# Seven products instead of eight in the down projection of both MLPs of a two-layer trunk, with new rooms for its operands and groups of 4, 4, 3 and 3 pairs

## The chip, the cores and the metric

The kernel runs on one core of one Trainium2 chip. The metric is the device time of one execution in microseconds; lower is better. The median of three runs before the change is 2502.86 us (2498.45 to 2505.21).

## The reference

The model is one step of a two-layer encoder over 1024 prompt rows and 32 sample rows (T = 1056 rows of D = 1024 columns). Layer 0 has an mLSTM mixer, layer 1 band attention over shared keys and values, and each layer has an MLP with a squared ReLU. All of it is in float32. Cut to what matters here:

```python
for l in range(DEPTH):                       # DEPTH = 2
    sh1, sc1, g1, sh2, sc2, g2 = jnp.split(ada_mod(c, p['w_ada'][l], p['b_ada'][l])[:, None, :], 6, axis=-1)
    u = x * (1 + sc1) + sh1
    ...
    x = layer_norm(ALPHA * x + (1 + g1) * y, p['ln_g'][l, 0], p['ln_b'][l, 0])
    u = x * (1 + sc2) + sh2
    f = jnp.square(jax.nn.relu(u @ p['w_up'][l])) @ p['w_down'][l]
    x = layer_norm(ALPHA * x + (1 + g2) * f, p['ln_g'][l, 1], p['ln_b'][l, 1])
```

`w_up[l]` is 1024 by 4096 and `w_down[l]` 4096 by 1024. `ada_mod` is the conditioning: silu(c) times a weight of 1024 by 6144 for each layer, for the prompt's and the sample's condition.

## The kernel before, in words

Data lie transposed: 128 features on the partitions, the 1056 rows along the free axis. A float32 product is made of three matmuls on values split into a high and a low part (`proj`, L118 high by high, L119 high by low, L120 low by high). `split` makes the two parts: ScalarE copies the high part (L89), VectorE subtracts for the low one (L90). Weights come from DRAM through three "raw" buffers and become split weights in six "wc" buffers of the pool `ring`; VectorE and ScalarE make them.

An accumulator holds the residual stream. In layer 0 it is three tiles of 384, 384 and 288 rows (`acc`, the blocks `TBS`); in layer 1 it is one tile (`ACC`). `add_gated_at` (L963) takes a finished PSUM bank, multiplies it by the gate and adds it to the accumulator, on VectorE. It makes one instruction for each piece of the accumulator and for each side of the border between prompt and sample, which lies at row 1024.

`Flow` runs side work in small steps: generators such as `norm` (a layer norm with its modulation) and `ada_rest` yield the number of ticks until their next step, and the main work calls `flow.tick` after each tile. `ada_rest` computes layer 1's conditioning while layer 0's MLP runs, in 32 pairs of 128 columns: for each pair two loads of 512 KB into raw buffers, 16 operations on VectorE (L238, L241), a transposition (L245) and a reduction (L246). The delays between its steps are `ADA_B`.

Layer 0's MLP (`mlp`) goes by 8 groups of 512 hidden features. In turn it makes `up` for a group (L1000 to L1003: ReLU and square, then the split into `h`) and `down` (four k blocks of the group, then `add_gated_at` into `acc`). It takes the rows in the three blocks of `TBS`, and the last group ends block by block, so that the next norm can begin.

Layer 1's MLP is written out by itself and takes down in another way. The rows are four quarters of 264 (`QN`), in two pairs `tp`; the hidden features are 16 pairs of 128-wide blocks. For 14 of them (`NW`) a two-by-two product of blocks (two quarters of rows, two blocks of hidden features, two blocks of outputs) is made with seven block products instead of eight (`PRODS`), from sums and differences of the blocks:

- `up_tile` puts ReLU and square of four tiles into `H` and makes the seven forms of the moving operand, split, in `HL`, of which there is one buffer. Two DMAs write HL to DRAM (`hd`).
- `forms` loads a block of `w_down` and makes the seven forms of the weights.
- `unit` is one group of pairs and one pair of outputs `m`: for each product 3 x kg matmuls of 264 columns (L1568) into one of three PSUM banks for a pair of quarters, and after each product an addition into the accumulator. The bank goes on collecting after that addition. Where `m` is 0 or 3 the two pairs of quarters follow each other, else they take turns.
- `load_f` (L1551) loads a form of the moving operand from `hd` into its room, 14 rooms in all; at `m == 3` it loads the next group's form after each product.

Groups have 3, 4, 4 and 3 pairs. The first group begins with extra units, because nine of its fourteen rooms come only after `HL`'s pool is closed. The last two pairs of hidden features are taken in the plain way at the end, block by block, with the final norm behind each block.

The order of TensorE's instructions in the attention and in layer 1's units is as written (`manual_schedule`); elsewhere, and on the other engines everywhere, a scheduler orders the instructions when the program is built. All loads and stores are issued by SyncE, in one queue.

Of the kernel before, what the change touches and what calls it, by code (L numbers as in the profile page):

```python
# [15 lines left out]
P = 128  # L16
# [59 lines left out]
def trunk_kernel(ctx: ExitStack, tc: tile.TileContext, a, o):  # L76
# [736 lines left out]
    ADA_B = (4.0, 2.0, 1.0)  # L813
# [7 lines left out]
    def make_layer(acc, pp, uo, usegs=segs):  # L821
# [4 lines left out]
        def norm(ti, ni, nm, w, affine=True, after=None):  # L826
# [48 lines left out]
            for i in range(0, KC, 2):  # L875
                nc.vector.tensor_mul(x[:, i:i + 2], x[:, i:i + 2], w2[:, 0:1].broadcast_to([P, 2, n]))
                for k in (i, i + 1):
                    for off, m, cnd in usegs(t0, n):
# [3 lines left out]
                                 tmp[:, :m], nc.scalar)  # L882
# [98 lines left out]
        def mlp(hp, l, gate, order, before_tb, after_tb, last):  # L981
            w_up, w_dn = a["w_up"][l], a["w_down"][l]
            NG = 8
            hs = {}
            wups = {}

            def up_w(g, pr):
                if (g, pr) not in wups:
                    wups[g, pr] = [wblock(f"up{l}_{g}_{pr}_{i}", w_up, 512 * i, g * 512 + pr * 256) for i in range(2)]
                return wups[g, pr]  # L990

            def up(g, c, ti):
                t0, n = TBS[ti]
                ps = mm(f"up_{l}_{g}_{c}_{t0}")
                proj(ps[:, :n], n, up_w(g, c // 2), c % 2, lambda hl, k: uo(hl, k, t0, n))
                if (g, c) not in hs:
                    hs[g, c] = hp.tile([P, 2, T], F32R, tag="h", name=f"h_{l}_{g}_{c}", bufs=5)
                ht = hs[g, c]
                r = tmp_t([P, 384], f"r_{l}_{g}_{c}_{t0}")[:, :n]
                nc.scalar.activation(r, ps[:, :n], AF.Relu)  # L1000
                nc.scalar.activation(ht[:, 0, t0:t0 + n], r, AF.Square)
                nc.vector.tensor_mul(r, r, r)
                nc.vector.tensor_sub(ht[:, 1, t0:t0 + n], r, ht[:, 0, t0:t0 + n].bitcast(F32))  # L1003
                flow.tick(n / 96)

            def down(g, w, fc, t0, n):
                ps = mm(f"dn_{l}_{g}_{fc}_{t0}")
                proj(ps[:, :n], n, [w], fc % 2, lambda hl, k: hs[g, k][:, hl, t0:t0 + n])
                add_gated_at(t0, n, ps, gate, fc)
                flow.tick(n / 192)  # L1010

            for pr in range(2):
                up_w(0, pr)
            early = set()
            for i, ti in enumerate(order):
                if i == 2:
                    for t in order[:EARLY]:
                        up(1, 0, t)
                        early.add(t)
                before_tb(ti)  # L1020
                for c in range(4):
                    up(0, c, ti)
            for g in range(NG):
                if g + 1 < NG:
                    for ti in order:
                        if g or ti not in early:
                            up(g + 1, 0, ti)
                if g < NG - 1:
                    for pr in range(4):
                        w = wblock(f"dn{l}_{g}_{pr}", w_dn, g * 512, pr * 256)  # L1030
                        for fc in (2 * pr, 2 * pr + 1):
                            for ti in order:
                                down(g, w, fc, *TBS[ti])
                    if g < NG - 2 or last is not TBS:
                        for c in range(1, 4):
                            for ti in order:
                                up(g + 1, c, ti)
                else:
                    ws = []

                    def finish(blk):
                        for fc in range(KC):
# [4 lines left out]
                    if last is TBS:  # L1047
# [4 lines left out]
                        for c, ti in ((3, 1), (2, 2), (3, 2)):  # L1052
                            up(g, c, ti)
# [632 lines left out]
```

## Time and profile before

| | |
|---|---|
| median of three runs | 2502.86 us |
| the profiled execution, its own time | 2503.12 us |
| its span, first to last instruction | 2501.3 us |
| granted TensorE clock, mean | 0.991 |
| layer 0's MLP, on TensorE | 516.0 to 1264.6 us |
| layer 1's up | 1732.2 to 2113.9 us |
| layer 1's units of seven products | 2113.7 to 2432.8 us |
| layer 1's plain rest of down and the last norm | to the end |

The profile is that of one execution. Busy time of an engine says how much of a stretch it worked; whether it sets the end is read from what the other engines wait for there. A matmul's own duration is longer than the distance between two of them, because they are pipelined; so TensorE's pace is read from how many matmuls a stretch without idle time holds.

### The profile page before, as it was taken

To read this page: it belongs to the slowest core of one execution; us is meant where nothing else is said; L and a number is where in the kernel's file an instruction comes from. 1 tells how busy PE (TensorE), PEld (TensorE's weight loads), DVE (VectorE), ACT (ScalarE), POOL (GpSimd) and SP (SyncE) were. 2 spreads that over 40 slices of the span, in tenths; PEclk is the share of its full clock that TensorE was granted. 3 is DMA by queue.
4 is the path that set the end of the run, shared out by engine and by line. 5 is a ranking of instruction groups with operands and counts; after the bars stand their busy time and mean duration, and the time that the engine had idled before them with its cause. 6 is when DMAs were issued, how large, how long until landed. Compare 5 with 4: busy or idle time off the path is not lost.

```text
span 2501.3 us, 42666 instructions
## 1 busy us (share of the span) xinstructions
PE 2418.5 (97%) x16844; PEld 2315.5 (93%) x16844; DVE 1755.0 (70%) x4033; ACT 1040.4 (42%) x2185; POOL 167.4 (7%) x315
## 2 busy tenths in 40 slices
PE   7999999999999999999999899998999999989997
PEld 4999999999999999999999877798999999889997
DVE  4899998778778768766696667737644442766678
ACT  4644455481221221221375566737944443211122
POOL 0211100000000000000001144400000000000003
PEclk9999999999999999999999999999999999999999
DMA  8433234313324323333123400051486667567552
GB/s 295 120 109 100 84 90 132 98 35 118 92 87 126 93 90 121 93 93 115 59 89 94 107 1 2 18 146 43 149 261 209 213 200 247 179 239 285 185 177 70
DMA packets 256108, 316.78 MB, mean 127 GB/s; under 512 B 11160, under 2 KB 233516, under 8 KB 251812
## 3 DMA queue, kind: packets, MB, share of 16 engines
q1 hardware_dynamic: 255908, 314.07, 38.7%
q8 instruction: 132, 2.16, 0.4%
q14 instruction: 68, 0.56, 0.1%
HBM read 241.48 MB, written 74.91 MB: 126 GB/s over the span
## 4 chain that ended last, share of the span: by engine, by line
PE 78%; DVE 7%; DMA 6%; ACT 3%; issue 1%; POOL 0%; SPq 0%; DVEq 0%; ACTq 0%; POOLq 0%
PE up L118 10%; PE up L119 10%; PE up L120 10%; PE dn L1568 8%; PE dn L119 5%; PE dn L118 5%; PE dn L120 5%; PE pv L1308 2%; PE pt L1288 2%; PE s L1258 2%; DMA fx_w<-hd 2%; DMA fx<-hd 1%; PE o L118 1%; PE o L119 1%; PE o L120 1%
## 5 line engine op out<-in xcount | busy, mean ns | idle before, releaser
L1568 PE MATMUL dn<-fx,wf 128*128 128x264 f32 x2184 | 276.7, 286 | 21.0 <-DMA fx<-hd 12.7
L1568 PEld LDWEIGHTS dn<-fx,wf 128*128 128x128 f32 x2184 | 270.4, 190 | 25.8 <-issue 10.9
L119 PE MATMUL up<-u,w_up 128*128 128x264 f32 x1024 | 290.8, 285 | 0.6 <-DVE u L331 0.6
L120 PE MATMUL up<-u,w_up 128*128 128x264 f32 x1024 | 290.0, 285 | 0.0
L118 PE MATMUL up<-u,w_up 128*128 128x264 f32 x1024 | 289.1, 286 | 0.2 <-ACT w_up L89 0.2
L119 PE MATMUL dn<-h,w_dn 128*128 128x384 f32 (+1 forms) x768 | 249.5, 325 | 0.0
L118 PE MATMUL up<-U,w_up 128*128 128x384 f32 (+1 forms) x768 | 249.2, 324 | 0.0
L119 PE MATMUL up<-U,w_up 128*128 128x384 f32 (+1 forms) x768 | 247.9, 323 | 0.0
L118 PE MATMUL dn<-h,w_dn 128*128 128x384 f32 (+1 forms) x768 | 247.8, 323 | 0.0
L120 PE MATMUL up<-U,w_up 128*128 128x384 f32 (+1 forms) x768 | 247.6, 322 | 0.0
L120 PE MATMUL dn<-h,w_dn 128*128 128x384 f32 (+1 forms) x768 | 247.3, 322 | 0.0
L963 DVE SCALAR_TENSOR_TENSOR ACC<-dn,ada,ACC 128x264 f32<-128x264 f32 (+5 forms) x328 | 133.1, 427 | 105.5 <-PE dn L1568 96.6
L119 PEld LDWEIGHTS up<-u,w_up 128*128 128x128 f32 x1024 | 194.5, 190 | 1.1 <-DVE u L331 1.1
L118 PEld LDWEIGHTS up<-u,w_up 128*128 128x128 f32 x1024 | 193.4, 190 | 0.6 <-ACT w_up L89 0.6
L120 PEld LDWEIGHTS up<-u,w_up 128*128 128x128 f32 x1024 | 193.3, 189 | 0.3 <-DVE w_up L90 0.3
L238 DVE SCALAR_TENSOR_TENSOR aacc<-rada,cs,aacc 128x256 f32<-128x256 f32 x448 | 190.3, 477 | 0.0
L963 DVE SCALAR_TENSOR_TENSOR acc<-dn,ada,acc 128x384 f32<-128x384 f32 (+2 forms) x256 | 119.3, 486 | 47.0 <-PE dn L120 45.9
L1000 ACT ACTIVATE r<-up 128x384 f32<-128x384 f32 (+1 forms) x96 | 44.2, 462 | 244.5 <-PE up L120 236.7
L119 PEld LDWEIGHTS dn<-h,w_dn 128*128 128x128 f32 x768 | 144.5, 188 | 0.2 <-DVE h L1003 0.2
L120 PEld LDWEIGHTS dn<-h,w_dn 128*128 128x128 f32 x768 | 144.5, 188 | 0.0
L120 PEld LDWEIGHTS up<-U,w_up 128*128 128x128 f32 x768 | 144.3, 188 | 0.0
L118 PEld LDWEIGHTS up<-U,w_up 128*128 128x128 f32 x768 | 144.2, 188 | 0.1
(350 smaller groups left out, 5986.6 us busy)
## 6 DMA issues: line engine op xcount, KB each, us to landing
hd<-HL SPq DMA_DIRECT2D x56, 924.0 KB
rada<-in_w_ada_dram SPq DMA_DIRECT2D x64, 512.0 KB
raw_up<-in_w_up_dram SPq DMA_DIRECT2D x64, 512.0 KB
fx<-hd SPq DMA_DIRECT2D x26, 1056.0 KB
fx<-hd SPq DMA_DIRECT2D x26, 792.0 KB
raw_dn<-in_w_down_dram SPq DMA_DIRECT2D x36, 512.0 KB
ada_room<-in_w_ada_dram SPq DMA_DIRECT2D x32, 512.0 KB
rada<-in_w_ada_kv_dram SPq DMA_DIRECT2D x16, 512.0 KB
```

The costliest lines, as they stand in the source:

```text
L118: nc.tensor.matmul(ps, wh, mov(0, k), start=(k == 0), stop=False)
L119: nc.tensor.matmul(ps, wh, mov(1, k), start=False, stop=False)
L120: nc.tensor.matmul(ps, wl, mov(0, k), start=False, stop=(k == nk - 1))
L238: nc.vector.scalar_tensor_tensor(acc[:, cnd], raw[:, k], sc, acc[:, cnd], op0=ALU.mult, op1=ALU.add)
L963: nc.vector.scalar_tensor_tensor(xs, ps[:, off + o:off + o + mm_], gate[:, fc, cnd:cnd + 1], xs, op0=ALU.mult, op1=ALU.add)
L1000: nc.scalar.activation(r, ps[:, :n], AF.Relu)
L1258: nc.tensor.matmul(s[:, b, :w], qst, kk[i][:, g, k0 + j0:k0 + j0 + w], start=(i == 0), stop=(i == 1))
L1288: nc.tensor.transpose(pt[:kp, j - j0, pr * P:(pr + 1) * P], ps_[pr][:, j * P:j * P + kp], ident)
L1308: nc.tensor.matmul(pv[64 * e:64 * e + 64, :nq], V[:kp, vt0 + j, g * 64:(g + 1) * 64], pts[e][:kp, j, :nq], start=(j == 0), stop=(j == nt - 1))
L1568: nc.tensor.matmul(p, ws[w][:, wl, k], x[:, xl, k], start=first and k + n_ == 0, stop=k == kg - 1 and n_ == 2, skip_group_check=not first)
```

## The change

A function `mlp7` takes the place of `mlp` and of layer 1's written-out MLP, and both layers use it, through classes `L0` and `L1` that tell it their operands and accumulators. `ADA_B` grows, and the low part of a modulation is made from a VectorE product in layer 1. `PRODS`, `forms` and `up_tile` are as before, apart from names; `up_plain` makes the last two pairs without `H` and `HL`. Cut to its core:

```diff
-    ADA_B = (4.0, 2.0, 1.0)
+    ADA_B = (5.0, 2.5, 1.0)
...
-                                 tmp[:, :m], nc.scalar)
+                                 tmp[:, :m], nc.scalar if usegs is segs else None)
...
-        def mlp(hp, l, gate, order, before_tb, after_tb, last):
...
+    GRP = [(0, 4), (4, 4), (8, 3), (11, 3)]
...
+    class Room:
+        def mov(self, hl, k):
+            return self.t[:, hl, k] if self.pieces is None else self.pieces(hl, k // 2)[:, k % 2 * QN:(k % 2 + 1) * QN]
+        def load(self, src, kg):
+            if self.pieces is None:
+                nc.sync.dma_start(self.t[:, :, :kg].bitcast(F32), src)
+                return
+            for hl in range(2):
+                for k in range(0, kg, 2):
+                    n = min(2, kg - k)
+                    nc.sync.dma_start(self.pieces(hl, k // 2)[:, :n * QN].bitcast(F32),
+                                      src[:, hl, k:k + n].rearrange("p k t -> p (k t)"))
+
+    def mlp7(L):
...
+        def up_plain(pb, tp):
+            for f in range(2):
+                r = tmp_t([P, 2, QN], f"hr{l}_{pb}_{f}_{tp}")
+                for i in range(2):
+                    nc.scalar.activation(r[:, i], up_mm(pb, f, 2 * tp + i), AF.Relu)
+                    flow.tick(QN / 96)
+                nc.vector.tensor_mul(r, r, r)
+                hl = ring.tile([P, 2, 2, QN], F32R, tag="raw", name=f"hl{l}_{pb}_{f}_{tp}", bufs=3)
+                split(hl[:, 0], hl[:, 1], r)
+                nc.sync.dma_start(hpl[2 * (pb - NW) + f, :, :, 2 * tp * QN:2 * (tp + 1) * QN],
+                                  hl.bitcast(F32).rearrange("p l q t -> p l (q t)"))
+        tp0, tp1 = L.pairs
+        for pb in range(2):
+            up_w(pb)
+        for i in range(2):
+            L.ready(i)
+            for pb in range(2):
+                for f in range(2):
+                    up_tile(pb, f, L.quarters[i])
+        up_unit(2, tp0)
+        L.ready(2)
+        for pb in range(3):
+            up_unit(pb, tp1)
+        for pb in range(3, NW):
+            for tp in L.pairs:
+                up_unit(pb, tp)
+        hh_cm.__exit__(None, None, None)
+        f4_cm = tc.tile_pool(name=f"f4{l}", bufs=1, reuse_waits="tile")
+        f4p = f4_cm.__enter__()
...
+        def unit(g, m, phases, ws, step, after):
...
+                        L.add((2 * tp + q) * QN, QN, p, L.gate, 2 * m + c)
+                        after(tp, f)
+                        flow.tick(QN * kg / 768)
...
+        units = [(g, m, [(tp0,), (tp1,)] if m in (0, 3) else [(tp0, tp1)]) for g in range(len(GRP)) for m in range(4)]
...
+        fill(rooms)
+        for tp in L.pairs:
+            for pb in range(NW, NPB):
+                up_plain(pb, tp)
+            if tp == tp0:
+                fill(L.rooms(tp0))
+                prep(0)
+        for _ in range(4):
+            got[0] = next(preps[0])
+        fill(L.rooms(tp1))
+        fill([Room(ring.tile([P, 2, KG, QN], F32R, tag="wc", name=f"fx_w{l}", bufs=6))])
...
+        hs = [f4p.tile([P, 2, T], F32R, tag=f"f4{c}", name=f"hs_{l}_{c}") for c in range(4)]
...
+        for t0, n in L.blocks:
+            for fc in range(KC):
+                ps = mm(f"dn{l}_{fc}_{t0}")
+                proj(ps[:, :n], n, [ws[fc // 2]], fc % 2, lambda hl, k: hs[k][:, hl, t0:t0 + n])
+                L.add(t0, n, ps, L.gate, fc)
+                flow.tick(n / 192)
+            L.after((t0, n))
...
+    class L0:
+        l, alloc, add, gate = 0, mm, add_gated_at, ada_part(0, 5)
+        pairs, quarters, blocks = (0, 1), (0, 1, 2, 3), TBS
+        ready, after = before0, end0
+        def rooms(pr):
+            return [Room(None, lambda hl, k2, i=i: U4[:, hl, 2 * i + k2, 2 * pr * QN:2 * (pr + 1) * QN])
+                    for i in range(4)]
+    mlp7(L0)
...
-    GRP = [(0, 3), (3, 4), (7, 4), (11, 3)]
...
-    units = [(0, 0, [(1,)]), (0, 1, [(1,), (0,)]), (0, 0, [(0,)]), (0, 2, [(1, 0)]), (0, 3, [(1,), (0,)])]
-    for g in range(1, len(GRP)):
-        units += [(g, m, [(1,), (0,)] if m in (0, 3) else [(1, 0)]) for m in range(4)]
...
-    room = u2_room(3) + u2_room(2) + [f1p.tile([P, 2, KG, QN], F32R, name="fx_1")]
...
+    class L1:
+        l, alloc, add, gate = 1, mm, add_gated_at, ada_part(1, 5)
+        order, blocks = rev, [(0, 288), (288, 256), (544, 256), (800, 256)]
+        pairs, quarters = (1, 0), (3, 2, 1, 0)
...
+    mlp7(L1)
```

The pool `f4` takes `HL`'s place after the fourteenth pair, so five of the fourteen rooms (one tile of its own and the four of `f4`) can be loaded while the plain pairs of up run. Four more per pair of quarters come from the input of up, as soon as up has read it for the last time: in layer 1 the tiles `u2`, in layer 0 pieces of the tile `U`, where one form lies in four pieces and takes four loads. The last room is a "wc" buffer.

More of the change, by code (lines that the diff above doesn't have):

```diff
@@ L1602, in trunk_kernel @@
-    for tp, fs in ((1, order_f[5:]), (0, order_f)):
-        for f in fs:
-            fx[tp, f] = room.pop(0)
-            load_f(0, tp, f)
-    with tc.manual_schedule(engines={mybir.EngineType.PE}):
-        for i, (g, m, phases) in enumerate(units):
-            prep(i + 1)
-            def step(j):
-                if i + 1 in preps and j in (0, 1, 3, 5):
-                    ready[i + 1] = next(preps[i + 1])
-            def after(tp, f):
-                if m == 3 and g + 1 < len(GRP):
-                    load_f(g + 1, tp, f)
-            unit(g, m, phases, ready[i], step, after)
```

416 lines of the change are left out of this document (170 added, 246 removed).

## The prediction

> **What bounds the kernel now.** I read the page first, then busy time by stage, then what TensorE waited for in layer 1's down, and last the prices of VectorE's instructions.
>
> ```profile
> span 2501.3 us, 42666 instructions
> PE 2418.5 (97%) x16844; PEld 2315.5 (93%) x16844; DVE 1755.0 (70%) x4033; ACT 1040.4 (42%) x2185; POOL 167.4 (7%) x315
> ```
>
> TensorE is busy 97% of the span. That alone doesn't say that it sets the end everywhere, so here are the stages. The columns after each window's length are busy us (and instructions) of PE, weight loads, DVE, ACT and POOL, then the granted clock, the DMA share and GB/s.
>
> ```profile
> 516.00:1264.60 748.60, 748.60 (x4684) 746.24 (x4684) 556.27 (x1195) 204.10 (x354) 0.00 (x0) 1.00 0.30 93
> 560.00:620.00 60.00, 60.00 (x392) 60.00 (x391) 53.18 (x120) 13.40 (x23) 0.00 (x0) 1.00 0.40 122
> 1732.20:2113.90 381.70, 377.80 (x3078) 376.51 (x3079) 182.38 (x250) 208.53 (x347) 0.00 (x0) 0.99 0.62 205
> 1830.00:1930.00 100.00, 100.00 (x830) 100.00 (x829) 43.76 (x55) 46.46 (x73) 0.00 (x0) 1.00 0.68 222
> 2113.90:2431.70 317.80, 294.91 (x2350) 289.47 (x2350) 210.06 (x462) 64.65 (x118) 0.00 (x0) 0.98 0.59 220
> 2114.00:2151.00 37.00, 26.85 (x188) 25.63 (x187) 20.80 (x50) 8.95 (x17) 0.00 (x0) 0.86 0.68 249
> 2203.00:2220.00 17.00, 11.81 (x87) 10.66 (x87) 3.02 (x7) 0.49 (x1) 0.00 (x0) 1.00 0.92 365
> 2300.00:2320.00 20.00, 17.45 (x140) 17.11 (x141) 14.32 (x28) 4.65 (x9) 0.00 (x0) 1.00 0.51 180
> 2431.70:2501.00 69.30, 55.42 (x460) 54.38 (x459) 54.23 (x137) 16.15 (x35) 20.11 (x14) 0.94 0.22 78
> ```
>
> The first row is layer 0's whole MLP: 748.6 us, PE never idle, 4608 of the 4684 matmuls its own, so 162.5 ns for one (of 384 columns twice and 288 once). The third to the fifth are layer 1: up, down in seven products, and the plain rest. The fourth gives the undisturbed pace of a 264-column matmul: 100 / 830 = 120.5 ns. Layer 1's down has 2352 matmuls of that shape, 283.4 us at that pace, and takes 317.8: 34 us are lost. The sixth row holds 14.3 of them (188 x 0.1205 = 22.7 of 37 us, at a clock of 0.86), the seventh 6.5 and the eighth 3.1. What TensorE waited for there:
>
> ```profile
> PE dn L1568 <- DMA fx<-hd: 12.7, 11, 5.1
> PE dn L1568 <- DVE ACC L963: 7.6, 9, 3.0
> PE dn L1568 <- DMA fx_w<-hd: 1.9, 2, 0.9
> ```
>
> So in layer 1 operands that come late cost most, and VectorE's additions into ACC less. In layer 0 TensorE alone sets the end, with VectorE close behind: 53.18 of 60 us in the second row.
>
> **The change: what TensorE gains.** In layer 0, up goes from 2304 matmuls to 3072 of 264 columns: 3072 x 0.1205 = 370.2 against 2304 x 0.1625 = 374.4. Down goes from 2304 to 2352 of 264 columns and 288 plain ones: 283.4 + 288 x 0.1625 = 46.8, together 330.2 against 374.4. By TensorE alone layer 0 would take 700.4 instead of 748.6, 48 us less. This is the whole intended gain; the question is who keeps pace with it.
>
> **What VectorE has to do in layer 0's down.** Prices (busy, mean ns of one, idle before):
>
> ```profile
> L238 DVE SCALAR_TENSOR_TENSOR aacc<-rada,cs,aacc 128x256 f32<-128x256 f32 x448 | 190.3, 477 | 0.0
> L241 DVE TENSOR_SCALAR aacc<-rada,cs 128x256 f32<-128x256 f32 x64 | 19.9, 342 | 0.0
> L245 DVE STREAM_TRANSPOSE aat<-aacc 128x512 f32<-128x512 f32 x32 | 22.6, 706 | 0.3
> L246 DVE TENSOR_REDUCE cx<-aat 128x16 f32<-128x512 f32 x32 | 21.7, 678 | 0.2
> L963 DVE SCALAR_TENSOR_TENSOR ACC<-dn,ada,ACC 128x264 f32<-128x264 f32 x160 | 77.9, 490 | 72.4 <-PE dn L1568 71.7
> L963 DVE SCALAR_TENSOR_TENSOR ACC<-dn,ada,ACC 128x232 f32<-128x232 f32 x64 | 29.2, 456 | 25.1 <-PE dn L1568 25.0
> L963 DVE SCALAR_TENSOR_TENSOR ACC<-dn,ada,ACC 128x32 f32<-128x32 f32 x72 | 17.4, 242 | 0.0
> L90 DVE TENSOR_TENSOR wf<-s,wf 128x512 fp32r<-128x512 f32 x32 | 20.6, 686 | 1.9 <-ACT wf L89 1.8
> L90 DVE TENSOR_TENSOR wf<-s,wf 128x384 fp32r<-128x384 f32 x36 | 18.4, 553 | 8.2 <-ACT wf L89 7.5
> L1535 DVE TENSOR_TENSOR s<-rdn,rdn 128x512 f32<-128x512 f32 x8 | 5.5, 686 | 2.6 <-DMA rdn<-in_w_down_dram 2.6
> L1535 DVE TENSOR_TENSOR s<-rdn,rdn 128x384 f32<-128x384 f32 x9 | 5.0, 557 | 8.8 <-DMA rdn<-in_w_down_dram 8.7
> ```
>
> These overlap when nothing stands between them:
>
> ```profile
> 646.93 2.46 DVE L238 SCALAR_TENSOR_TENSOR aacc<-rada,cs,aacc 128x256 f32<-128x256 f32 x6
> ```
>
> Six instructions of 477 ns took 2.46 us, (2.46 - 0.477) / 5 = 397 ns from start to start. So each occupies the engine some 0.08 us less than its mean, and I take that off every price. [...] The row shows the overlap, so the sum goes by the row.
>
> The instruction order of the changed program has, between the first and the last addition of layer 0's units, three kinds of work on VectorE:
> - 400 additions. Layer 0's accumulator lies in pieces of 384, 384 and 288 columns, so three of the four quarters are cut by a seam or by the prompt's end (120+144, 240+24, 232+32); only 48 additions have 264 columns. The cut ones lie on the line through the 32- and 232-column rows (0.242 and 0.456, 1.07 ns a column): 48 x 0.408 and 176 pairs of 0.530 to 0.534, 113.6 us.
> - 174 operations for the weight forms, 86 of 512 columns (0.604) and 88 of 384 (0.470): 93.4 us.
> - Half of layer 1's conditioning, 16 of its 32 column pairs (14 of L238, 2 of L241, one each of L245 and L246, 7.2 us for a pair): 113.9 us. The new delays (5.0, 2.5, 1.0) and the ticks in the units spread it over up and down. Before, up and down took turns in eight groups and it lay beside both, 556 of 748.6 us in layer 0's row.
>
> Together 321 us against TensorE's 283. So layer 0's down turns from TensorE's stage into VectorE's. How far it goes beyond 321 depends on how evenly the work lies between the additions, since a product's bank can't be written again before its addition. Taking the larger of TensorE's and VectorE's work unit by unit gives 327, in threes of products 364, product by product 410. The same count for layer 1's down of before exceeds TensorE's work by 8 us in threes; the trace shows 7.6 us of waits for ACC. I take the threes, 364, and 4 us for operands at changes of group: 368, with 327 and 410 as ends. ACT isn't near: 64.65 of 317.8 us in layer 1's down, and no conditioning runs on it.
>
> **Layer 0's up.** TensorE needs 370.2; layer 1's up, with the same code, took 381.7. One loop in it has little to spare, the buffer HL, of which there is one:
>
> ```profile
> 1865.23 0.41 ACT L89 CAST HL<-H 128x264 fp32r<-128x264 f32 x1 [4.18 <-DMA hd<-HL]
> 1877.39 0.41 ACT L89 CAST HL<-H 128x264 fp32r<-128x264 f32 x1 [5.56 <-DMA hd<-HL]
> ```
>
> From one use to the next it takes 12.16 us, the last 5.56 spent by ACT on the landing of HL's write, against 96 x 0.1205 = 11.6 us of TensorE's work for one use. In layer 0 the conditioning adds VectorE work between HL's two splits (1.6 us on average in the new order against 0.7 in layer 1's, partly beside ACT's copy), and its weights share the DMA engines:
>
> ```profile
> rada<-in_w_ada_dram SPq DMA_DIRECT2D x64, 512.0 KB
> fx<-hd SPq DMA_DIRECT2D x26, 1056.0 KB
> ```
>
> 16 pairs of two loads over 28 uses are 0.6 MB a use, 1.6 us at the seventh window's 365 GB/s. Bounds: 370 when all of it hides, and 28 x (12.16 + 0.9 + 1.6) + 4 x 11.6 = 457 when both add wholly. I take 386, near layer 1's row, since TensorE there ran at full pace with the loop as tight. VectorE as a whole isn't the bound of up: layer 1's 182 us and 16 pairs, 115, make 297 of 386.
>
> Around it: norms enter up by quarters and end the plain part. The only row for that is layer 1's up, 3.9 us idle of 381.7; I add 3, with 0 and 8 as ends. Layer 0: 386 + 368 + 46.8 + 3 = 804, against 748.6: 55 us more.
>
> **Layer 1.** Its products are the same 2352. Of the first group's fourteen operand loads nine instead of five now have their room before up ends, which removes most of the loss in down's first 37 us: 14.3 becomes 3. Groups of 4, 4, 3, 3 put the change 3 to 4, with 15.1 MB of loads (14 of 1056 KB, the second row above; 41 us at 365 GB/s) behind 35 us of work, out of the way: 6.5 becomes about 3 at 4 to 4 (as the eighth row), nothing at 4 to 3, some 2 at 3 to 3. That is 18 us less, with 0 and 30 (all of the loss but VectorE's waits) as ends. The first form of weights is made once instead of twice, beside TensorE's work. The second half of each modulation goes from ACT to VectorE, in the norms before up: bounded by the 3.9 us idle there, I take 2. The plain pairs of up leave HL's loop for a shorter path, under TensorE's work: nothing. The tail's loads change rooms only; VectorE has 54 of 69 us there, unchanged: nothing.
>
> SP issues 38 loads at a change of group in layer 0 instead of 14, since rooms cut out of U take four each:
>
> ```profile
> 1860.35 1.79 SPq L96 DMA_DIRECT2D raw_up<-in_w_up_dram  x2
> ```
>
> Two issues in 1.79 us make 34 us for 38, under the 45 of a slowed unit pair; nothing is added, up to 5 us a change if loads queue behind them.
>
> Sum: the profiled execution's own 2503.1 (span 2501.3) + 55 - 20 = 2538; that execution is 0.3 above the median of the three runs.
>
> **The rivals.**
> - VectorE's lag is absorbed (ends faster). Layer 0's down goes at TensorE's pace with layer 1's old 15 us of operand waits, 298; up 372; with 46.8 and 3, 720 in all, 28 less; with layer 1's 20 less, 2455. For it: VectorE at 89% in the second row cost TensorE nothing. Against it: 321 of occupied time doesn't fit 298; it needs some 25 us of the conditioning to run earlier than its place in the order. It decides where VectorE's work in the units falls under TensorE's 283.
> - HL's loop binds layer 0's up, each use waiting for the conditioning's weights too: 28 x 13.8 + 46 = 432, 46 over the forecast, 2584. For it: ACT's 5.56 us on the landing. Against it: 830 matmuls in 100 us beside that very wait.
> - The early rooms bring nothing in layer 1, because the loads queue behind what up writes (DMA share 0.62 in up): 18 us come back, 2556. Against it: five loads are 5.4 MB, 15 us at 365 GB/s, and have 46 us of plain up.
>
> **How the numbers follow.** Chances: the forecast 0.60, absorbed lag 0.14, HL 0.16, no gain in layer 1 0.10. The forecast's own range is 2505 (down 342, unit by unit and some waits) to 2575 (down 405). 8 in 10 lie between 2492 and 2590: below are most of the absorbed lag's cases, above HL with a slow down. About 0.3% (7.5 us) is what a measurement tells from no change: faster 0.14, within 0.07, slower 0.79.
>
> **What would show it.** Right: in layer 0's down VectorE busy over 90% and TensorE waiting for acc at L963's counterpart for 50 us or more, with the units of 3 (15.2 us of matmuls) at about 19 us; up near 385; in layer 1 the first 37 us of down without the dip. Wrong: layer 0's down under 320 us, or TensorE waiting there mostly for loads or forms instead of additions; or up over 420, which would be HL. A conditioning that ends before down would upset the sum itself.

## The result, and the profile after

The changed kernel takes 2633.45 us, median of four runs (2630.65 to 2637.28), against 2504.03 for the kernel before on the same chip: a ratio of 1.0521, 95% interval 1.0504 to 1.0538. It is slower, by 129 us where 35 were forecast, and above the range. The profiled execution took 2630.9 us. From its page, the span and the busy times:

```profile
span 2629.1 us, 45783 instructions
PE 2427.5 (92%) x17948; PEld 2317.1 (88%) x17948; DVE 1873.5 (71%) x4378; ACT 1087.2 (41%) x2234; POOL 165.8 (6%) x315
```

TensorE is busy about as long as before (2427.5 against 2418.5 us) in a span that is 127.8 longer: it now waits. The 48 us that it was to save in layer 0 don't show, for the most part because some of its work ran at a slow pace, as told below. The windows by stage, columns as in the prediction: up and units of layer 0, the units' first 29 us, the first change of group, the plain rest, the q stage (from the first product of layer 1's q to the last), then layer 1's up, its units and their first 37 us.

```profile
514.80:911.00 396.20, 378.24 (x3102) 376.85 (x3100) 277.04 (x518) 183.53 (x312) 0.00 (x0) 0.97 0.75 243
911.00:1312.80 401.80, 324.42 (x2384) 315.52 (x2384) 337.78 (x888) 64.88 (x119) 0.00 (x0) 0.90 0.58 202
911.00:940.00 29.00, 10.26 (x50) 9.61 (x51) 18.78 (x39) 6.49 (x13) 0.00 (x0) 0.63 0.72 249
1005.00:1065.00 60.00, 49.57 (x391) 48.73 (x391) 40.32 (x111) 6.10 (x10) 0.00 (x0) 0.94 0.86 315
1312.80:1363.00 50.20, 49.84 (x303) 49.25 (x304) 42.40 (x73) 16.73 (x24) 0.00 (x0) 0.97 0.28 91
1363.00:1482.00 119.00, 100.55 (x586) 97.82 (x585) 80.55 (x148) 71.45 (x145) 5.97 (x3) 0.91 0.30 95
1853.80:2259.10 405.30, 380.87 (x3079) 379.89 (x3079) 190.72 (x284) 195.08 (x311) 0.00 (x0) 0.96 0.61 204
2259.10:2560.60 301.50, 290.59 (x2359) 287.21 (x2358) 210.89 (x464) 61.24 (x114) 0.00 (x0) 1.00 0.58 217
2259.00:2296.00 37.00, 33.25 (x271) 32.71 (x270) 26.75 (x55) 10.59 (x19) 0.00 (x0) 1.00 0.73 268
```

The q stage of the kernel before, for comparison:

```profile
1264.60:1360.40 95.80, 95.08 (x585) 93.53 (x584) 78.02 (x142) 62.64 (x134) 6.96 (x3) 1.00 0.30 94
```

Layer 0's MLP takes 848.2 us (748.6 before), the q stage 119.0 (95.8), layer 1's up 405.3 (381.7), its units 301.5 (317.8); the plain rest with the last norm 68.4 (69.3); everything between is unchanged. That is 99.6 + 23.2 + 23.6 - 16.3 - 0.9 = 129.2, less 1.2 by which layer 0 begins sooner: 128, the whole difference.

In layer 0's units TensorE is idle for 401.8 - 324.42 = 77.4 us. What ends that time, in us, times and the longest:

```profile
PE dn L1159 <- DVE acc L963: 34.6, 20, 5.8
PE dn L1159 <- ACT wf L89: 14.8, 4, 12.1
PE adas L252 <- DVE cx L246: 12.7, 4, 5.2
PE dn L1159 <- DVE wf L90: 6.0, 4, 2.7
```

The busy part is slow too: 2384 matmuls at 120.5 ns are 287 us, and they took 324, at a granted clock of 0.90. So the units' 402 us are 287 of work, 77 of waiting and 37 of slow pace. Their first 29 us alone hold only 50 matmuls, 6 us of work.

VectorE isn't busy throughout either, 337.78 of 401.8 us. Most of its idle 64 us it waits for TensorE's products:

```profile
DVE acc L963 <- PE dn L1159: 53.5, 66, 3.1
```

TensorE's rows in up show a wait that the forecast hadn't, and a slow pace behind it (start, duration, and in brackets the idle time before and what ended it):

```profile
876.41 0.59 PE L118 MATMUL up<-U,w_up 128*128 128x264 f32 x1 [17.83 <-ACT w_up L89]
...
877.02 0.42 PE L118 MATMUL up<-U,w_up 128*128 128x264 f32 x1
877.24 0.42 PE L119 MATMUL up<-U,w_up 128*128 128x264 f32 x1
...
881.14 0.29 PE L120 MATMUL up<-U,w_up 128*128 128x264 f32 x1
881.27 0.28 PE L118 MATMUL up<-U,w_up 128*128 128x264 f32 x1
```

TensorE stands 17.83 us for the weights of up's last pair. Then matmuls start 220 ns apart and last about 0.42 us until 881.14; from there on they start 120 ns apart and last 0.28 to 0.29 us. In layer 1 the same wait takes 18.6 us, at 2222. SyncE's queue tells why:

```profile
857.46 2.47 SPq L1005 DMA_DIRECT2D fx<-hd  x4
861.20 0.56 SPq L1080 DMA_DIRECT2D hpl<-hl  x1
861.80 1.79 SPq L96 DMA_DIRECT2D raw_up<-in_w_up_dram  x2
873.89 0.37 SPq L231 DMA_DIRECT2D rada<-in_w_ada_dram  x1
```

The two loads of the last weights (raw_up) are issued behind four loads into the new early rooms (fx) and a store of halves that had to be made first. The early rooms do get their loads while up runs, and up pays for it.

### The profile page after: what moved, and what is told of

The parts are those of the page before. It is cut to its first block, busy times and chain, and to the rows that moved or that the text cites. A ratio compares the mean times of both kernels' runs of the same rounds, so it can differ in the third digit from the quotient of the medians.

```text
span 2629.1 us, 45783 instructions
## 1 busy us (share of the span) xinstructions
PE 2427.5 (92%) x17948; PEld 2317.1 (88%) x17948; DVE 1873.5 (71%) x4378; ACT 1087.2 (41%) x2234; POOL 165.8 (6%) x315
## 4 chain that ended last, share of the span: by engine, by line
PE 57%; DVE 20%; DMA 12%; ACT 4%; issue 2%; SPq 0%; POOL 0%; ACTq 0%; DVEq 0%; POOLq 0%
PE dn L1159 15%; PE up L118 5%; PE up L119 5%; PE up L120 5%; DMA hd<-HL 4%; DVE aacc L238 4%; PE pv L1487 2%; DVE HL L90 2%; PE pt L1467 2%; DMA raw_up<-in_w_up_dram 2%; DVE wf L90 2%; DVE acc L963 2%; PE s L1437 2%; DMA fx_w<-hd 2%; DMA rada<-in_w_ada_dram 1%
## 5 line engine op out<-in xcount | busy, mean ns | idle before, releaser
L1159 PE MATMUL dn<-fx,wf 128*128 128x264 f32 x3024 | 401.0, 292 | 49.1 <-ACT wf L89 16.1
L1159 PEld LDWEIGHTS dn<-fx,wf 128*128 128x128 f32 x3024 | 387.8, 195 | 56.5 <-ACT wf L89 27.4
L118 PE MATMUL up<-u,w_up 128*128 128x264 f32 x1024 | 291.4, 287 | 18.6 <-ACT w_up L89 18.6
L118 PE MATMUL up<-U,w_up 128*128 128x264 f32 x1024 | 291.7, 286 | 17.8 <-ACT w_up L89 17.8
L119 PE MATMUL up<-U,w_up 128*128 128x264 f32 x1024 | 291.4, 285 | 0.1
L120 PE MATMUL up<-U,w_up 128*128 128x264 f32 x1024 | 290.1, 284 | 0.0
L118 PEld LDWEIGHTS up<-U,w_up 128*128 128x128 f32 x1024 | 192.9, 189 | 18.2 <-ACT w_up L89 18.0
L1159 PE MATMUL dn<-U,wf 128*128 128x264 f32 x1344 | 185.0, 296 | 20.9 <-DVE acc L963 19.3
L90 DVE TENSOR_TENSOR HL<-H,HL 128x264 fp32r<-128x264 f32 x112 | 125.2, 1118 | 106.3 <-ACT HL L89 106.0
L1159 PEld LDWEIGHTS dn<-U,wf 128*128 128x128 f32 x1344 | 177.8, 199 | 24.3 <-DVE acc L963 22.0
L963 DVE SCALAR_TENSOR_TENSOR ACC<-dn,ada,ACC 128x264 f32<-128x264 f32 (+4 forms) x328 | 133.9, 427 | 88.8 <-PE dn L1159 79.9
L119 PEld LDWEIGHTS up<-U,w_up 128*128 128x128 f32 x1024 | 193.3, 189 | 0.3 <-DVE U L331 0.3
L120 PEld LDWEIGHTS up<-U,w_up 128*128 128x128 f32 x1024 | 193.3, 189 | 0.1
L963 DVE SCALAR_TENSOR_TENSOR acc<-dn,ada,acc 128x144 f32<-128x144 f32 (+8 forms) x432 | 144.1, 372 | 62.0 <-PE dn L1159 53.5
L89 ACT CAST HL<-H 128x264 fp32r<-128x264 f32 x112 | 107.3, 965 | 170.2 <-DMA hd<-HL 133.4
```

Source lines behind the costliest of these rows:

```text
L89: nc.scalar.copy(dst_h, src)
L90: (eng or nc.vector).tensor_sub(dst_l, src, dst_h.bitcast(F32))
L118: nc.tensor.matmul(ps, wh, mov(0, k), start=(k == 0), stop=False)
L119: nc.tensor.matmul(ps, wh, mov(1, k), start=False, stop=False)
L120: nc.tensor.matmul(ps, wl, mov(0, k), start=False, stop=(k == nk - 1))
L963: nc.vector.scalar_tensor_tensor(xs, ps[:, off + o:off + o + mm_], gate[:, fc, cnd:cnd + 1], xs, op0=ALU.mult, op1=ALU.add)
```

## The experiments

Medians are compared with 2633.45 for the changed kernel and with the kernel before as measured beside each run (2503 to 2506).

**Up's last weights ahead of the early rooms.**

```diff
+        for pb in range(NW, NPB):
+            up_w(pb)
         fill(rooms)
```

> The weights of up's last pair are loaded ahead of the early rooms' loads. Theory (they wait behind the four fx loads and the hl buffers of the shared raw ring): the gaps of 17.8 us in layer 0's up and 18.6 us in layer 1's up fall to under 4 us each, about 2598 us against 2633. Rival (the plain pairs wait for HL's last writes or for the rooms themselves): the gap only moves to another instruction, over 2620 us.

2610.53 us, ratio 1.0417 (1.0392 to 1.0441), 23 us faster than the changed kernel. Both layers' up, in windows of this run:

```profile
517.50:893.40 375.90, 375.78 (x3102) 374.71 (x3100) 274.76 (x515) 181.53 (x310) 0.00 (x0) 1.00 0.76 245
1847.70:2231.00 383.30, 376.84 (x3080) 375.86 (x3080) 186.78 (x278) 191.76 (x306) 0.00 (x0) 0.99 0.64 213
```

Both waits are gone, and layer 0's up runs at full clock with TensorE never idle: 3072 matmuls in 375.9 us, so HL's loop doesn't bind there. But only layer 1 keeps most of its gain (up, units and the rest to the end take 759.1 us against 775.3). In layer 0 the units are 12.7 us longer: at the first unit TensorE now waits 16.5 us for the conditioning's statistics, where it had waited 5.2. The theory holds for the wait, and the rival for most of what layer 0 would have gained; the time lies between the two.

**Without the conditioning's products**, seven eighths of them left out, loads kept.

```diff
+                        if light and (half or k):
+                            continue
                         if half or k:
```

> Layer 1's conditioning keeps its loads and its first 128 of 1024 inputs but leaves out the other products (448 L238 of VectorE). Theory (VectorE's conditioning work holds layer 0's units, and the idle it makes throttles TensorE's clock): the units fall from 396 us to 295 to 315, granted clock there back to 0.98 or more, waits for acc from 38 to under 10 us, 2525 to 2550 us in all. Rival (the cut-up rooms in U with their four loads, or the 25 instead of 18 additions for a unit): the units stay over 350 us.

**And without seven eighths of its loads too.**

```diff
+                if light and half:
+                    continue
...
-                nc.sync.dma_start(raw, src[512 * half:512 * half + 512, ...
+                nk = 1 if light else 4
+                nc.sync.dma_start(raw[:, :nk], src[512 * half:512 * half + 128 * nk, ...
```

> The run without most of the conditioning's products once more, its loads left out as well (one eighth of them is kept). Theory: what was left of the units there (348 us over TensorE's 283) is partly the conditioning's 17 MB of loads, which share SyncE's queue and the DMA engines with the forms at the changes of group; then the units take 315 to 335 us. Rival: the forms' own bytes (14 times 1.1 MB for each change) and the first unit's late weights make it; then they stay at 342 to 352.

2576.65 and 2553.13 us, one run each. The units of the first:

```profile
908.00:1256.00 348.00, 302.75 (x2353) 295.88 (x2352) 250.18 (x646) 63.70 (x117) 0.00 (x0) 0.94 0.68 233
```

and of the second, with its first 24 us:

```profile
921.00:1252.40 331.40, 298.07 (x2335) 292.81 (x2334) 230.66 (x596) 63.24 (x117) 0.00 (x0) 0.95 0.58 202
921.00:945.00 24.00, 12.53 (x81) 12.01 (x80) 13.22 (x27) 5.07 (x9) 0.00 (x0) 0.72 0.93 318
```

Read against the changed kernel, the conditioning's products cost the units 401.8 - 348.0 = 54 us, its loads 348.0 - 331.4 = 17. The first run lands between theory and rival, close to the rival (its units' granted clock is 0.94 with 45 us of idle time on TensorE, 0.90 with 77 in the changed kernel), and the second within its theory: VectorE's work for the conditioning is the largest single item, but not all. Of the 48 us left over TensorE's 283, 24.0 - 81 x 0.1205 = 14 lie at the first unit, where the DMA engines are busy for 0.93 of the time.

**The norms' steps due in half the time.**

```diff
-    W01 = (6.0, 12.0, 3.0, 3.0, 3.0)
+    W01 = (3.0, 6.0, 1.5, 1.5, 1.5)
```

> The delays between the steps of layer 0's last norms are halved. Theory (the norms' steps fall due too late, because the plain part ticks half as fast and now ends the MLP in one piece): the q stage falls from 119 us to 100 to 107, 2615 to 2622 us in all. Rival (the norms' own chain on VectorE and ACT sets it, about 14 us from mean to variance): no change, 2629 to 2638.

2635.89 us, ratio 1.0532 (1.0512 to 1.0553), nothing gained; the q stage stays at 121.7 us. Due times aren't why it is long; that theory fell.

**The kernel before, with its last three up products ahead of block 0's down.**

```diff
-                        for c, ti in ((1, 0), (1, 1), (1, 2), (2, 0), (3, 0), (2, 1)):
+                        for c, ti in ((1, 0), (1, 1), (1, 2), (2, 0), (3, 0), (2, 1), (3, 1), (2, 2), (3, 2)):
                             up(g, c, ti)
                         finish(last[0])
-                        for c, ti in ((3, 1), (2, 2), (3, 2)):
-                            up(g, c, ti)
```

> The kernel before, with layer 0's last three up products (3,1), (2,2), (3,2) computed ahead of block 0's down instead of behind it; the same work, in another order. Theory: the 23 us by which the q stage is longer in the changed kernel (119.0 against 95.9) are cover that was lost: in the kernel before some 12 us of up stand between the end of block 0's down and block 1's, and the norms' statistics run behind them; then this kernel's q stage takes 105 to 120 us and the time is 2513 to 2530. Rival: the stage is longer because VectorE comes out of the units behind TensorE, or because of the norms' due times; then the order of these three products costs nothing here, the q stage stays at 94 to 99 and the time within 4 us of the kernel before.

2509.2 us, ratio 1.0019 (1.0010 to 1.0029). The q stage takes 99.5 us here: lost cover is worth 4 us of the 23. That theory fell for the most part. But this run has the norms' statistics at about the same distance from the first product of q as the changed kernel has, and still is 19 us shorter, so the difference had to lie in what TensorE's order holds behind them. In the changed kernel 48 matmuls of q stand ahead of block 2's variance, here 172, and TensorE waits 12.3 us at that point. SyncE's queue in the changed kernel points to a reason:

```profile
1315.83 0.34 SPq L302 DMA_DIRECT2D tab<-in_rel_bias_b_dram  x1
1321.53 0.37 SPq L96 DMA_DIRECT2D raw_q<-in_w_q_b_dram  x1
1322.44 0.33 SPq L309 DMA_DIRECT2D e_d<-rev  x1
1322.86 0.38 SPq L96 DMA_DIRECT2D raw_q<-in_w_q_b_dram  x1
1325.30 0.60 SPq L311 DMA_DIRECT2D bias_d<-e_d  x1
1372.88 0.58 SPq L1263 DMA_DIRECT2D xsp<-acc  x1
1373.51 3.31 SPq L96 DMA_DIRECT2D raw_q<-in_w_q_b_dram  x3
```

q's third weights (raw_q) are issued 51 us behind its second, behind block 0's store (xsp), which waits for the norm. Between them lie the three transfers of a small table (tab, e_d, bias_d). The late issue alone doesn't make it: in the run with the norms' steps halved the third weights are issued at 1360.74, before the stage begins, and it is as long; there too 48 matmuls of q stand ahead of the long wait (15.3 us).

**The bias table early.** `bias_table` uses two tiles of the ring of raw weights. It follows the conditioning, which before ended at 1158 us and now ends with the units, so these tiles fall between down's last weights and q's.

```diff
         combine(2, lng(2), lnb(2), ada_part(1, 4), ada_part(1, 3))
-        yield
-        bias_table()
...
             norms["ada"] = flow.add(ada_rest())
+            bias_table()
```

> The changed kernel with the bias table (two small tiles in the ring of raw weights, three loads) made at the start of layer 0's up, when the conditioning is set going, instead of behind the conditioning's end. Theory: the q stage is 23 us longer because the conditioning now ends with the units, so that the bias table's tiles stand in the ring of raw weights between down's last weights and q's; the third of q's weights is then issued only behind block 0's store at 1373.5, TensorE's order has no products of q to put before block 2's statistics, and it waits 12.3 us there. Then the q stage takes 96 to 103 us here instead of 119.0, the units stay at 398 to 405, and the time is 2611 to 2620. Rival: the stage is long because VectorE and ScalarE are late with block 1's and 2's norms; then it stays above 114, and the time above 2627.

2614.92 us, ratio 1.0431 (1.0416 to 1.0447), 18.5 faster than the changed kernel; its q stage:

```profile
1365.70:1465.20 99.50, 96.60 (x586) 95.19 (x585) 80.07 (x148) 68.84 (x144) 6.48 (x3) 0.98 0.30 93
```

Shown: 19.5 of the 23 us come from the place of the table, three small transfers and two tiles of a ring. Which of these does it, by way of the order that the scheduler then builds, isn't separated.

**Two loads instead of four for a form in U.**

```diff
-            for hl in range(2):
-                for k in range(0, kg, 2):
-                    n = min(2, kg - k)
-                    nc.sync.dma_start(self.pieces(hl, k // 2)[:, :n * QN].bitcast(F32),
-                                      src[:, hl, k:k + n].rearrange("p k t -> p (k t)"))
+            rows = U4[:, :, self.r0:self.r0 + 2, self.c0:self.c0 + 2 * QN].bitcast(F32)
+            for i in range(2):
+                if kg == 4:
+                    nc.sync.dma_start(rows[:, i], src[:, i].rearrange("p (a k) t -> p a (k t)", k=2))
...
```

> The changed kernel with each form that goes into a room of U loaded by two DMAs instead of four; the same bytes. Theory: SyncE's queue is what layer 0's units wait for at the start and at the changes of group: 32 loads into U take it 27.7 us at a change, and the weights of the next unit stand behind them; with 16 loads a change it is done some 12 us sooner, the units of layer 0 take 370 to 388 us instead of 401.8, and the time is 2610 to 2624. Rival: the bytes are the limit (14 forms of 1.1 MB in the 25 us of a unit), or an issue takes as long as its rows; then a load into U takes twice as long to issue, the units stay at 396 to 405 and the time is above 2626.

2637.85 us, ratio 1.0524 (1.0509 to 1.0538). At the first change of group SyncE issues 20 loads in the changed kernel like this:

```profile
1018.37 19.20 SPq L1010 DMA_DIRECT2D U<-hd  x20
```

and 10 of twice the size in this run like this:

```profile
1025.74 14.46 SPq L1010 DMA_DIRECT2D U<-hd  x10
```

That is 0.96 and 1.45 us for one. The theory fell: the units take 401 us here. The rival's time holds, though one load takes half as long again, not twice as long. So the number of loads doesn't set the time; that the bytes do is argued, not shown.

**Three moves together**: up's last weights early, the bias table early, and the first unit's weights ahead of the loads into U's first rooms.

```diff
             if tp == tp0:
-                fill(L.rooms(tp0))
                 prep(0)
+                fill(L.rooms(tp0))
```

> The changed kernel with three moves: up's last weights issued ahead of the loads into the early rooms (both layers), the first unit's weights issued ahead of the loads into U's first rooms, and the bias table early. Theory: each takes its own wait away: 23 us (measured by itself), 12 us (TensorE's wait for the first unit's last forms) and 16 us: 2578 to 2590. Rival: the wait at the first unit is VectorE's backlog (conditioning and splits), not the late weights; then 10 us or more of wait stay between 890 and 940, and the time is 2592 to 2602.

2581.99 us, ratio 1.0295 (1.0269 to 1.0322). The time is the theory's, the reason isn't: 16.8 and 12.1 us of wait stay between 890 and 940, as the rival said. The two moves measured alone make 41 of the 51 us; what the third did is not shown.

**More of the conditioning in up**: the three moves with `ADA_B = (3.5, 1.5, 1.0)`.

> The same with the conditioning's steps at (3.5, 1.5, 1.0), so that three quarters of its pairs fall into up and a quarter into the units. Theory: conditioning costs its VectorE time in the units (53 us for half of it) and is nearly free in up, where VectorE is busy 277 of 396 us: the units get 20 to 30 us shorter and up at most 8 longer, so this is 12 to 28 us faster than the run with the three moves. Rival: up's VectorE is as full as the units' (H, its splits and the conditioning come in bursts), and what the units give up takes: within 8 us of that run, or slower.

2592.8 us, ratio 1.0344 (1.0323 to 1.0365), 11 slower. The edit missed its aim: a step falls due in whole ticks, 2.75 in up, so 3.5 takes two ticks as 5.0 does, and 15 pairs are done within up in both runs. It only pressed the rest together in the units. So once more, with steps counted in ticks:

```diff
-    ADA_B = (5.0, 2.5, 1.0)
+    ADA_B = [2.75, 2.75, 2.75]
...
+        ADA_B[:] = [5.0, 5.0, 2.5]
         with tc.manual_schedule(engines={mybir.EngineType.PE}):
```

> The run with the three moves, with the conditioning's steps at (2.75, 2.75, 2.75) while up runs and (5, 5, 2.5) in the units. Steps fall due in whole ticks (2.75 in up), so the steps of the last run moved no pair, and the split stayed at 16 pairs in up and 17 behind it; these put 22 in up and 10 or 11 behind. Theory: the pairs cost the units 53 us for 16, 3.3 each, and are free in up: six pairs fewer shorten the units by 15 to 22 us and the time is 2559 to 2568. Rival: up pays (its VectorE work comes in bursts, and the conditioning's loads take turns with up's weights in one ring of three), 5 us or more there, or the units wait for something else: 2574 or more.

2551.3 us, ratio 1.0190 (1.0176 to 1.0204). The two stages with the three moves alone, units first:

```profile
891.10:1303.20 412.10, 324.28 (x2384) 315.51 (x2384) 336.70 (x884) 63.81 (x118) 0.00 (x0) 0.89 0.60 206
515.00:891.00 376.00, 376.00 (x3103) 374.82 (x3102) 276.00 (x519) 182.42 (x312) 0.00 (x0) 1.00 0.78 254
```

and with six pairs more in up:

```profile
516.00:894.00 378.00, 376.90 (x3115) 374.89 (x3113) 317.72 (x636) 181.46 (x308) 0.00 (x0) 1.00 0.83 266
894.00:1274.00 380.00, 308.73 (x2349) 300.67 (x2350) 298.45 (x773) 67.10 (x124) 0.00 (x0) 0.91 0.61 211
894.00:935.00 41.00, 6.12 (x25) 5.07 (x26) 18.88 (x39) 6.43 (x14) 0.00 (x0) 0.55 0.83 290
```

Up pays 2.0 us, the units get 32 shorter: more than the theory's 22, and the rival is out. The pairs left in the units also stand further apart here (11 in 319 us, with the three moves alone 16 in 412), so the 32 us are not the price of six pairs alone. In up VectorE now works 317.72 of 378 us, and TensorE doesn't notice. What is left at the first unit can be seen in VectorE's rows of this run:

```profile
904.00 0.49 DVE L963 SCALAR_TENSOR_TENSOR acc<-dn,ada,acc 128x264 f32<-128x264 f32 x1 [2.26 <-PE dn L1159]
915.36 0.61 DVE L241 TENSOR_SCALAR aacc<-rada,cs 128x256 f32<-128x256 f32 x2 [10.87 <-DMA rada<-in_w_ada_dram]
...
927.60 3.25 DVE L238 SCALAR_TENSOR_TENSOR aacc<-rada,cs,aacc 128x256 f32<-128x256 f32 x8 [7.40 <-DMA rada<-in_w_ada_dram]
...
931.52 0.65 DVE L1126 TENSOR_TENSOR s<-rdn,rdn 128x512 f32<-128x512 f32 x1
```

VectorE stands 10.87 and 7.40 us at the conditioning's data (rada), whose loads are queued behind loads into U, and the sums for the next forms (s) stand behind it; TensorE's waits in these units begin with:

```profile
PE dn L1159 <- ACT wf L89: 34.9, 5, 30.7
PE dn L1159 <- DVE acc L963: 17.5, 11, 3.4
```

The first unit's forms (wf) hold it up for 30.7 us at once; waits for additions are half of the changed kernel's.

**The conditioning held while up's last pairs run, and their halves in another ring** (the run before, with the units' steps at (4, 4, 1)).

```diff
                     nc.scalar.activation(r[:, i], up_mm(pb, f, 2 * tp + i), AF.Relu)
-                    flow.tick(QN / 96)
...
-                hl = ring.tile([P, 2, 2, QN], F32R, tag="raw", name=f"hl{l}_{pb}_{f}_{tp}", bufs=3)
+                hl = ring.tile([P, 2, 2, QN], F32R, tag="wc", name=f"hl{l}_{pb}_{f}_{tp}", bufs=6)
```

> The same, and at the start of the units: up's last two pairs put their halves into the ring of finished weights instead of that of raw weights, and the conditioning does not step while these two pairs run, so that its loads and the halves' stores no longer stand between the loads into U, and the first unit's weights are issued ahead of all loads into U (units' steps (4, 4, 1)). Theory: the 29 us that TensorE waits between up's end and the second unit (16.8 for the conditioning's statistics, 12.1 for forms) come from one queue: loads behind loads into U, and VectorE standing at the conditioning's data with the forms' sums behind it. At most 8 us of it stay, and the run is 16 to 24 us faster than the one with the new steps alone. Rival: these waits are VectorE's and ScalarE's own work of the first forms and of the last halves; then 18 us or more stay, and the gain is under 9 us.

2556.38 us, ratio 1.0216 (1.0201 to 1.0232). The wait at the first unit goes from 32.8 us (30.7 and 2.0) to 14.4 (11.2 and 3.2), but the time doesn't: TensorE's waits for additions go from 17.5 to 33.2, and for the conditioning's statistics from 5.3 to 17.2. So the theory fell in the time, and 14.4 us stay where it allowed 8. Three things were changed at once, so how much of this is due to the denser steps stays open.

**The halves' stores on GpSimd's queue**, else the same.

```diff
-                nc.sync.dma_start(hpl[2 * (pb - NW) + f, :, :, 2 * tp * QN:2 * (tp + 1) * QN],
+                nc.gpsimd.dma_start(hpl[2 * (pb - NW) + f, :, :, 2 * tp * QN:2 * (tp + 1) * QN],
```

> The run before last once more, with one thing changed: the stores of up's last halves are issued on GpSimd's queue instead of SyncE's. Theory: the 14.4 us that TensorE still waits at the first unit there come from ScalarE, which stands at the halves' room (12.8 us ahead of a cast at 891.2) until their stores, queued on SyncE behind loads into U, are done, with the casts of the first forms behind it; then at most 6 us of wait stay and the time is 2540 to 2550. Rival: it is the DMA engines that are full with the loads into U, whichever queue the stores are on, or the first forms' own work: 11 us or more stay, and the time is 2552 or more.

2556.11 us, ratio 1.0199 (1.0182 to 1.0216); 11.2 us of wait for forms stay, and 9.1 us for an addition come soon after. The window of the first unit:

```profile
893.00:920.00 27.00, 15.76 (x111) 14.97 (x111) 16.72 (x38) 8.60 (x18) 2.77 (x4) 0.75 1.05 404
```

The DMA engines are full in both runs: a share of 1.05 by the records and 404 GB/s here, 0.98 and 356 GB/s from 892 to 920 us with the stores on SyncE's queue. The theory fell and the rival holds: 9 of the first group's 14 forms have no room before up has read its input, and then all of them come at once. How much the first forms' own work adds isn't separated.

**Layer 1 alone changed**, layer 0's MLP and `ADA_B` as before.

> Layer 0 as before the change (with the delays 4, 2, 1), layer 1 as after. Theory (layer 1 wins 17 us in its units and loses 24 in up, 18.6 of them in one gap): 2508 to 2513 us, a little slower than before. Rival (layer 1's up is slow only because of what layer 0 left behind): up back at 382, about 2487 us.

2514.06 us, ratio 1.0039 (1.0024 to 1.0054), 1 us above the theory's range and far from the rival; up takes 406.7 us here too. Layer 0 makes 119 of the 129 us. Then with up's last weights early:

> Layer 0 as before, layer 1 changed, and in layer 1 the weights of up's last pairs issued ahead of the loads into the early rooms. Theory: the 19.5 us in which layer 1's up waits for its last weights go, some 4 us come back at the first unit as they did with both layers changed: 2496 to 2503, faster than the kernel before by 0.1 to 0.4%. Rival: the loads that now come later hold the first unit up by as much: 2510 or more.

2497.37 us, ratio 0.9972 (0.9961 to 0.9983), as the theory said. With the modulation back on ScalarE:

```diff
-                                 tmp[:, :m], nc.scalar if usegs is segs else None)
+                                 tmp[:, :m], nc.scalar)
```

> The same, with the second modulation of layer 1's norms back on ScalarE, as in the kernel before. Theory: moving it to VectorE lengthened the three gaps ahead of layer 1's up from 6.1 to 9.5 us, so this is 1 to 5 us faster than the run with the move. Rival (what the prediction took): the move is worth 2 us, so this is 1 to 3 us slower.

2494.26 us, ratio 0.9958 (0.9946 to 0.9971). It points to the theory's side by 3 us, but the intervals overlap. And with the halves in the ring of finished weights:

> Layer 1 alone changed, with the weights of up's last pairs early, the norms' modulation on ScalarE, and the halves of up's last pairs in the ring of finished weights. Theory: the 5.0 us in which layer 1's first unit waits for its first form go, since its weights are issued ahead: 2487 to 2492. Rival: the ring of finished weights is full there, and its own wait takes their place: 2493 or more.

2489.93 us, ratio 0.9944 (0.9931 to 0.9956), in the theory's range: 14 us faster than the kernel before, the version that beats both. The wait at the first unit goes from 5.0 to 2.4 us; against the run above the intervals overlap, so this last step isn't clear of noise. The first 37.5 us of its units:

```profile
2112.50:2150.00 37.50, 34.77 (x273) 34.50 (x273) 27.48 (x56) 12.03 (x22) 0.00 (x0) 0.95 0.63 228
```

273 matmuls, against 188 in 37 us before.

## Why the prediction was wrong, point by point

- **TensorE's work** was right: 375.9 us for layer 0's up without the wait (370 worked out, 386 forecast), 287 for the units.
- **VectorE binds the units** was right in kind and mis-sized in the term "the threes, 364, and 4 us for operands": 401.8, within the stated ends of 327 and 410. By the removals the conditioning makes 54 us, its loads 17, and 48 are left, 14 of them at the first unit. The sum took VectorE as busy throughout; it is busy 84%, not over 90%, since it waits 53.5 us for TensorE's products while TensorE at other times waits for it. Waits for acc are 34.6 us, not 50: the largest part of TensorE's 77, but less than half. The sum left out two things, which overlap: the 37 us of slow pace, most of it right behind waits (from 1165.16, 25 matmuls in 5.67 us instead of 3.0), and the first unit, where 50 matmuls take 29 us, so 23 are lost, and 4 stood for operands in all. That 287 of work and 77 of waiting make just the 364 of the threes is luck, since part of the waiting is for forms and for the conditioning's statistics.
- **"Nothing is added" for SyncE's loads.** The issue was right: the 38 loads of the first change of group take 33 us in SyncE's rows, 34 worked out. TensorE waits for loads into U only 1.5 us in all units. The change still takes 60 us for 391 matmuls (47 us), with the DMA engines at 0.86; TensorE waits there 7.4 us for additions, 2.0 for statistics and 1.1 for forms. How much of that the loads cause is not shown.
- **Up, 386**, came near in size (396.2) by luck: most of the 16 us over TensorE's work that it gave to HL and the conditioning didn't come, but 17.8 of waiting for the last weights did. Layer 1's 18.6 weren't in the sum at all. The prediction asked whether the early loads fit into the plain pairs' 46 us, not what stands behind them in the queue. This is the largest step missed in layer 1.
- **"Around it 3, with 0 and 8 as ends"** failed: 23 us in the q stage, 19.5 of them the bias table's place. The change doesn't touch the table's lines; the conditioning, which they follow, now ends later. The q stage had no term in the sum.
- **Layer 1's units** were right: -16.3 against -18, and their first 37 us have no dip (33.25 of 37 us busy). **The norms** were wrong: the waits for norms around the start of layer 1's up grew from 6.1 to 9.5 us, and a gain of 2 us from the move to VectorE is not seen.
- **The rivals.** An absorbed lag is out, HL's loop is out (375.9 at full clock), and the early rooms do bring their gain in layer 1.

The miss is 93 us: 34 in the units, 24 in layer 1's up, 20 in the q stage, 10 in layer 0's up, and the rest in small terms. The waits for up's last weights alone are 36 us (the rest of layer 0's up went 8 better than forecast), and the q stage's are 20, nearly all from the table's place; only the 34 lie where the prediction looked.

Whether layer 0 could come out ahead stays open: the best run with both layers changed (2551.3) is 54 us above the one with layer 1 alone and the same early weights (2497.4).

## What to carry to other kernels

Work that is worked off beside the main work has a place as well as a price: here six pairs of the conditioning moved out of the units, with the rest further apart, took 32 us from them and added 2 to up, and its end dragged a table behind it that held up another stage. Before a load is moved forward, list what is issued behind it in the same queue and in the same ring of buffers, and who waits for that first. Count delays in the ticks that really occur, since a smaller delay can be the same tick.

## What the runs showed of the hardware

Two waits of TensorE cost more than their length here. After the one of 17.83 us above, matmuls started 220 ns apart instead of 120 for 4.7 us. After one of 2.71 us the pace was about as low (changed kernel, TensorE's rows):

```profile
1165.16 1.91 PE L1159 MATMUL dn<-fx,wf 128*128 128x264 f32 x7 [2.71 <-DVE wf L90]
1166.87 2.18 PE L1159 MATMUL dn<-U,wf 128*128 128x264 f32 x9
1168.85 2.18 PE L1159 MATMUL dn<-fx,wf 128*128 128x264 f32 x9
1170.83 1.34 PE L1159 MATMUL dn<-U,wf 128*128 128x264 f32 x8
```

25 matmuls in 5.67 us, 227 ns each; from 1176.26 us on 9 took 1.08 us, 120 ns each. After a wait of 1.99 us that ended at 1015.69 the pace stayed near the full one: the 12 matmuls from 1015.89 on took 1.72 us. What decides whether the pace falls after a wait is not shown.
